# Half of the attention probabilities turned by VectorE's blocks and DMAs in place of TensorE

## The chip, the cores and the metric

The program runs on one core of a Trainium2 chip. The metric is the device time of one execution in microseconds (us). A core has five engines with an instruction queue each: TensorE (PE; its weight loads are shown as PEld), VectorE (DVE), ScalarE (ACT), GpSimd (POOL) and SyncE (SP, which here only issues DMAs). They run at the same time and wait for each other through semaphores. Operands lie in SBUF; TensorE writes to PSUM, from which ScalarE and VectorE copy ("evacuate").

## The reference

One layer of a decoder on a sequence of 256 positions and a width of 1024. One input projection feeds eight softmax attention heads of width 64 (MoBA) and four heads of gated linear attention (GLA); their outputs go through an output projection, then a feed-forward part with a short convolution (ConvGLU).

```python
xn = rms_norm(x, attn_norm_g[l])
proj = xn @ w_in[l]
mq = rope(split_heads(proj[..., o_mq:o_mk], MOBA_HEADS), pos)
mk = rope(split_heads(proj[..., o_mk:o_mv], MOBA_HEADS), pos)
mv = split_heads(proj[..., o_mv:o_gq], MOBA_HEADS)
y_moba = merge_heads(moba_attention(mq, mk, mv))
...
og = gla_attention(gq, gk, gv, split_heads(log_a, GLA_HEADS))
...
x = x + jnp.concatenate([y_moba, y_gla], axis=-1) @ w_out[l]
hn = rms_norm(x, ffn_norm_g[l])
h = causal_dwconv(hn @ w_ffn_up[l], conv_w[l], conv_b[l])
h_gate, h_val = h[..., :D_FF], h[..., D_FF:]
x = x + (jax.nn.silu(h_gate) * h_val) @ w_ffn_down[l]
return rms_norm(x, final_norm_g)
```

With 256 positions there is one key block, so the MoBA attention is plain causal softmax attention: for each head, P = softmax(q k^T / 8) below the diagonal, and P v.

## The kernel before

All large products are computed with operands split in a high part (`hi`) and a rest (`lo`), three matmuls each (`mm3`, lines 116 to 118). The weights come in slots of 1 MB: SP loads `raw`, ACT rounds it to `hi` (L99), DVE subtracts to get `lo` (L102), and a load is issued when a `raw` buffer has been split. The order of work in the first third of the kernel is written out by hand. The projection is a sequence of 48 steps on TensorE (`steps`, indices 0 to 47; from 24 on a step takes 1.4 us), and 16 more steps do the output projection. `plan` gives at an index q, or half a step later, a list of pieces that are emitted there: the attention's small matmuls, the work of ACT and DVE, and the splits of coming slots. PE, ACT and DVE each carry out their instructions in the emitted order.

The attention works on four pairs of heads. `m_scores(pr)` computes the scores of a pair on TensorE into two PSUM buffers of the pool `att` (four buffers, used in rotation). The same buffers hold one level of the GLA's triangular product (`lvl_c`), copied out by DVE in `lvl_d_` (L410). For each head h, `m_max(h)` (DVE, L557) adds the mask, takes the row maximum and writes the negated scores to one of four buffers `pes`; `m_exp(h)` (ACT, L564) takes the exponential and its sum; `m_div(h)` divides by the sum, with a reciprocal on DVE (L570), the first 128 columns scaled on ACT (L571) and the other 256 on DVE (L572). A head's P has 384 columns: rows are queries, two query blocks of 64 in each half of the partitions, and only the part up to the diagonal is kept.

P has to be turned for the product with v. `m_pt(pr)` does that on TensorE: twelve transposes of 64x128 pieces for a pair (L581) into two `att` buffers, evacuated by ACT in four operations (L587, L588) to `pt`. `m_av(n)` multiplies v and pt of two pairs (L601, L602) into one `att` buffer, which ACT and DVE split into `mh` and `ml` (L606, L607), operands of the output projection. `lvl_last` and `g_av` do the like for the GLA, `g_norm` and `g_gated` give its `y`, and `g_out` turns y on TensorE (L499).

Each pair passes through these steps one plan entry after another: m_scores(1), m_pt(0) and the softmax of heads 2 and 3 at 33.5; m_scores(2), m_pt(1) and heads 4 and 5 at 36.5; m_scores(3), m_pt(2) and heads 6 and 7 at 40; m_pt(3) and then m_av(0), m_av(1) at 45.5. Later in the kernel, `blocks` and `to_rows` (L913, L920) turn another tensor, hT, by 32x32 blocks on DVE and sixteen DMAs from SBUF to SBUF.

Of the kernel before, what the change touches and what calls it, by code (L numbers as in the profile page):

```python
# [34 lines left out]
def trunk_kernel(ctx: ExitStack, tc: tile.TileContext, xT_d, wG_d, w5_d, wo_d, up_d, dn_d,  # L35
                 par_d, gla_g_d, fin_g_d, wgu_d, cos_d, sin_d, causal_d, lvl_d, ident_d, out_d):
    nc = tc.nc
    V, A, T, DMA = nc.vector, nc.scalar, nc.tensor, nc.sync
# [123 lines left out]
    ml = main.tile([128, KT, S], F32R, name="ml")  # L162
# [66 lines left out]
    gv = at.tile([128, 2, 512], F32, name="gv")  # L229
# [8 lines left out]
    st = {}  # L238
# [310 lines left out]
    pes = [at.tile([128, 448], F32, name=f"pe{i}") for i in range(4)]  # L549
    for pe in pes:  # L550
        nc.gpsimd.memset(pe[64:128, 384:448], 0.0)

    def m_max(h):
        p, pe = st["s", h], pes[h % 4]
        mx = at.tile([128, 8], F32, name="mx", bufs=4)
        for i, (a, b, c) in enumerate(((0, 128, 0), (64, 320, 128))):
            V.tensor_tensor_reduce(pe[:, c:c + b - a], p[:, a:b], causal[:, c:c + b - a], -(HD ** -0.5), 3e38,  # L557
                                   ALU.add, ALU.min, mx[:, i:i + 1])
        st["mx", h] = mx
# [8 lines left out]
    def m_div(h):  # L568
        mx, pe = st["mx", h], st["pe", h]
        V.reciprocal(mx[:, 6:8], mx[:, 4:6])  # L570
        A.activation(pe[:, 0:128], pe[:, 0:128], AF.Copy, scale=mx[:, 6:7])  # L571
        V.tensor_scalar(pe[:, 128:384], pe[:, 128:384], mx[:, 7:8], None, op0=ALU.mult)  # L572

    def m_pt(pr):

        p = [att() for _ in range(2)]
        for h in range(2):
            for c in range(3):
                for r, rs in enumerate(HALVES):
                    a = c * 128 + 64 * (r and c > 0)  # L580
                    T.transpose(p[r][:, (3 * h + c) * 64:(3 * h + c) * 64 + 64],  # L581
                                st["pe", 2 * pr + h][rs, a:a + 128], ident[rs, rs])
        pt = at.tile([128, 2, 384], F32, name="pt", bufs=4)
        for r in range(2):
            o = pt.rearrange("p h (c t) -> p h c t", c=3)
            i = p[r][:, :384].rearrange("p (h c t) -> p h c t", h=2, c=3)
            A.activation(o[:, :, 0, HALVES[r]], i[:, :, 0], AF.Copy)  # L587
            A.activation(o[:, :, 1:, HALVES[1 - r]], i[:, :, 1:], AF.Copy)  # L588
        st["pt", pr] = pt

    def m_av(n):

        p = att()
        for pr in (2 * n, 2 * n + 1):
            c = S * (pr % 2)
            for hh in range(2):
                h = 2 * pr + hh
                pt = st["pt", pr][:, hh]
                r = slice(64 * hh, 64 * hh + 64)
                vs = slice(64 * h, 64 * h + 64)  # L600
                T.matmul(p[r, c:c + S], mv[:, 0, vs], pt[:, 0:256], start=True, stop=False, skip_group_check=True)  # L601
                T.matmul(p[r, c + 128:c + 256], mv[:, 1, vs], pt[:, 256:384],  # L602
                         start=False, stop=True, skip_group_check=True)
        mh = st["mh"]
        pv = p.rearrange("p (a t) -> p a t", a=2)
        A.activation(mh[:, 2 * n:2 * n + 2], pv, AF.Copy)  # L606
# [24 lines left out]
    for q, f in (  # L631
            (2, lambda: do((xsplit, 6), (xsplit, 7), (xsq, 3), (galloc, 6), (ghi, 6), (glo, 6), (ghi, 7), (glo, 7))),
            (4, lambda: do((xadd, 3), (xsum,), (hi, 6, 0), (lo, 6, 0), (g_wgs_hi,), (hi, 7, 0))),
            (12, lambda: do((xnorm, lambda: slots[7].split_lo(0, 512)), (lambda: slots[7].split_lo(512, 1024),), (g_evac, 0), (g_lr_split,), (g_evac, 1), (g_wgs_lo,), (hi, 7, 1), (lo, 7, 1))),
            (12.5, lambda: do((DMA.dma_start, lvl, lvl_d), (masks,))),
            (13.5, lambda: do((hi, 8, 0))),
            (14.5, lambda: do((g_transpose_lr,), (g_transpose, 0), (g_transpose, 1), (xrow,), (lo, 8, 0), (g_diag,))),
            (15.5, lambda: do((g_gate_mm,), (g_gate,), (hi, 9, 0), (g_decay,), (lo, 9, 0), (hi, 9, 1))),
            (16.5, lambda: do((lvl_u, 0), (lo, 9, 1), (lvl_u, 1))),
            (18, lambda: do((rope_a, 0, 0), (rope_b, 0, 0), (hi, 10, 0), (lo, 10, 0), (rope_a, 0, 1), (rope_b, 0, 1), (hi, 10, 1), (lo, 10, 1))),  # L640
            (20, lambda: do((hi, 11, 0), (lo, 11, 0), (hi, 11, 1), (lvl_keep,), (DMA.dma_start, glag, gla_g_d))),
            (24, lambda: do((lvl_u, 2), (rope_a, 1, 0), (rope_b, 1, 0), (lo, 11, 1), (rope_a, 1, 1), (rope_b, 1, 1), (hi, 12, 0), (lo, 12, 0), (g_diag2, 0), (g_diag2, 4))),
            (29, lambda: do((hi, 12, 1), (lvl_first,), (m_scores, 0), (m_max, 0), (m_exp, 0), (m_max, 1), (m_exp, 1), (lvl_d_, 0), (lvl_d_, 1), (lvl_u, 3), (m_div, 0), (m_div, 1), (lvl_d_, 2), (lo, 12, 1), (hi, 13, 0), (lo, 13, 0))),
            (33.5, lambda: do((hi, 13, 1), (m_scores, 1), (m_pt, 0), (m_max, 2), (m_exp, 2), (m_max, 3), (m_exp, 3), (lvl_u, 4), (m_div, 2), (m_div, 3), (lo, 13, 1), (lvl_d_, 3), (mv_evac, 0), (mv_evac, 1), (hi, 14, 0), (lo, 14, 0))),
            (36.5, lambda: do((hi, 14, 1), (m_scores, 2), (m_pt, 1), (m_max, 4), (m_exp, 4), (m_max, 5), (m_exp, 5), (lvl_u, 5), (m_div, 4), (m_div, 5), (lo, 14, 1), (lvl_d_, 4))),
            (37, lambda: do((hi, 15, 0), (lo, 15, 0))),
            (40, lambda: do((hi, 15, 1), (m_scores, 3), (m_pt, 2), (m_max, 6), (m_exp, 6), (m_max, 7), (m_exp, 7), (lvl_u64,), (lvl_d_, 5), (m_div, 6), (m_div, 7), (lvl_join,), (lo, 15, 1))),
            (41, lambda: do((gv_evac, 0), (gv_evac, 1), (hi, 16, 0), (lo, 16, 0))),
            (42, lambda: do((hi, 16, 1), (lo, 16, 1))),
            (45.5, lambda: do((m_pt, 3), (lvl_last,), (lvl_last_d,), (m_av, 0), (m_av, 1), (g_av, 0), (g_av, 1), (hi, 17, 0), (lo, 17, 0), (hi, 17, 1), (lo, 17, 1))),  # L650
            (48, lambda: do((g_tail,), (hi, 18, 0), (lo, 18, 0), (hi, 18, 1), (lo, 18, 1))),
            (51, lambda: do((g_out,),)),
            (52, lambda: do((A.preload_act_table_set, "abs_reciprocal_sqrt_and_small"), (hi, 19, 0), (lo, 19, 0), (hi, 19, 1), (lo, 19, 1)))):
        on(q, f)
# [55 lines left out]
    for q, (g, k) in enumerate(steps):  # L710
# [464 lines left out]
```

## Time and profile before

| | before |
|---|---|
| time, median of 3 executions | 306.48 us (306.25 to 307.33) |
| the profiled execution | 306.11 us |
| its span in the profile | 304.1 us |
| TensorE busy | 297.7 us |
| TensorE's granted clock | 1.00 |
| VectorE busy | 248.2 us |
| ScalarE busy | 207.0 us |
| DMA | 56.38 MB, 185 GB/s |

The span runs from the first to the last instruction that the profile shows; the execution's own time lies around it. In the rows of the profile, a group or a piece is named by its line (L102 is line 102 of the kernel before), its engine, its operation and its tiles, output first, with partitions x elements. A row of the view in order of time begins with the start in the span and the duration, both in us; "[0.64 <-ACT hi L99]" says that the engine was idle for 0.64 us before it and what ended that. "xN" merges N equal instructions in a row.

### The profile page before, as it was taken

The numbers are of one execution on the slowest core, as the hardware profiler recorded it, in microseconds if no ns is written. First come the engines' busy times: TensorE is split into PE (matmuls) and PEld (weight loads), VectorE is DVE, ScalarE is ACT, GpSimd is POOL, SyncE is SP. The second block draws the span as 40 slices with busy tenths as digits, with TensorE's granted clock in tenths as the row PEclk, the third lists the DMA queues.
The fourth block names the chain that finished last, engine by engine and source line by source line (L and its number), as shares of the span: only waits on it lengthen the run. The fifth ranks groups of instructions, "written<-read, shape, count | busy, mean of one in ns | idle before, by whom it ended". The sixth has DMA issues, their size and how long they took to land.

```text
span 304.1 us, 6224 instructions
## 1 busy us (share of the span) xinstructions
PE 297.7 (98%) x2470; PEld 282.2 (93%) x2470; DVE 248.2 (82%) x464; ACT 207.0 (68%) x384; POOL 4.8 (2%) x21
## 2 busy tenths in 40 slices
PE   8999999999999999999999999999999999999992
PEld 8999988777889999999999999999999999999992
DVE  3788998999387699799999998887888788876653
ACT  3988999898998487657667775555556665534362
POOL 2020000000000000000000000000000000000000
PEclk9999999999999999999999999999999999999999
DMA  6998845274553542991567666448788622220003
GB/s 163 391 332 307 297 165 198 91 261 141 176 182 134 204 168 65 426 370 32 210 245 256 254 235 236 170 156 224 211 194 234 267 71 69 71 69 2 0 0 139
DMA packets 20892, 56.38 MB, mean 185 GB/s; under 512 B 9840, under 2 KB 11648, under 8 KB 16640
## 3 DMA queue, kind: packets, MB, share of 16 engines
q1 hardware_dynamic: 20720, 55.86, 53.1%
q8 instruction: 19, 0.31, 0.4%
q10 hardware_dynamic: 144, 0.13, 0.1%
q14 instruction: 9, 0.07, 0.1%
HBM read 53.89 MB, written 1.05 MB: 181 GB/s over the span
## 4 chain that ended last, share of the span: by engine, by line
PE 98%; ACT 0%; issue 0%; DVE 0%; ACTq 0%
PE att L116 14%; PE att L117 14%; PE att L118 14%; PE acc L116 14%; PE acc L118 14%; PE acc L117 14%; PE att L746 4%; PE acc L727 1%; PE att L77 1%; PE att L399 1%; PE att L535 1%; PE att L581 1%; PE att L463 1%; PE att L601 1%; PE acc L735 1%; PE att L302 0%
## 5 line engine op out<-in xcount | busy, mean ns | idle before, releaser
L99 ACT ACTIVATE hi<-raw 128x1024 fp32r<-128x1024 f32 (+4 forms) x87 | 79.9, 941 | 38.4 <-PE att L117 31.9
L102 DVE TENSOR_TENSOR lo<-raw,hi 128x1024 fp32r<-128x1024 f32 (+4 forms) x89 | 93.6, 1065 | 14.0 <-ACT hi L99 14.0
L116 PE MATMUL att<-hh,hi 128*128 128x256 f32 x352 | 98.4, 279 | 0.0
L117 PE MATMUL att<-hl,hi 128*128 128x256 f32 x352 | 98.3, 279 | 0.0
L118 PE MATMUL att<-hh,lo 128*128 128x256 f32 x352 | 98.2, 279 | 0.0
L116 PEld LDWEIGHTS att<-hh,hi 128*128 128x128 f32 x352 | 66.2, 188 | 0.0
L117 PEld LDWEIGHTS att<-hl,hi 128*128 128x128 f32 x352 | 66.2, 188 | 0.0
L118 PEld LDWEIGHTS att<-hh,lo 128*128 128x128 f32 x352 | 66.2, 188 | 0.0
L873 DVE SCALAR_TENSOR_TENSOR c<-us,par,c 128x256 f32<-128x256 f32 x88 | 40.7, 482 | 4.1 <-ACT c L865 2.5
L865 ACT ACTIVATE c<-us,par 128x256 f32<-128x256 f32 x44 | 24.0, 591 | 23.7 <-DVE us L855 18.4
L118 PE MATMUL acc<-dhi,gl 128*128 128x512 f32 (+1 forms) x88 | 32.1, 365 | 0.0
L117 PE MATMUL acc<-dlo,gh 128*128 128x512 f32 (+1 forms) x88 | 32.1, 365 | 0.0
L116 PE MATMUL acc<-dhi,gh 128*128 128x512 f32 (+1 forms) x88 | 31.9, 363 | 0.0
L815 DVE TENSOR_TENSOR dlo<-draw,dhi 128x1024 fp32r<-128x1024 f32 x22 | 26.6, 1218 | 0.0
L855 DVE TENSOR_TENSOR us<-att,rb 128x512 f32<-128x512 f32 x20 | 13.8, 688 | 11.5 <-PE att L118 11.5
L810 ACT ACTIVATE dhi<-draw 128x1024 fp32r<-128x1024 f32 x22 | 23.0, 1046 | 0.0
L116 PE MATMUL acc<-hi,ah 128*128 128x512 f32 x48 | 19.5, 406 | 0.0
L118 PE MATMUL acc<-hi,al 128*128 128x512 f32 x48 | 19.0, 396 | 0.0
L117 PE MATMUL acc<-lo,ah 128*128 128x512 f32 x48 | 19.0, 396 | 0.0
L117 PEld LDWEIGHTS acc<-dlo,gh 128*128 128x128 f32 x88 | 16.5, 188 | 2.0
L116 PEld LDWEIGHTS acc<-dhi,gh 128*128 128x128 f32 x88 | 16.5, 188 | 1.9
L118 PEld LDWEIGHTS acc<-dhi,gl 128*128 128x128 f32 x88 | 16.5, 188 | 1.9
(222 smaller groups left out, 511.0 us busy)
## 6 DMA issues: line engine op xcount, KB each, us to landing
raw<-in_up SPq DMA_DIRECT2D x22, 1024.0 KB, 4.9
draw<-in_dn SPq DMA_DIRECT2D x22, 512.0 KB, 5.7
raw<-in_w SPq DMA_DIRECT2D x7, 1024.0 KB, 6.8
raw<-in_wo SPq DMA_DIRECT2D x4, 1024.0 KB, 4.8
raw<-in_w SPq DMA_DIRECT2D x4, 512.0 KB, 5.6
raw<-in_wG SPq DMA_DIRECT2D x3, 528.0 KB, 5.8
raw<-in_w SPq DMA_DIRECT2D x4, 256.0 KB, 5.4
xg<-hB SPq DMA_DIRECT2D x16, 64.0 KB, 6.4
```

What stands on the lines that cost most here:

```text
L77: T.matmul(wp[:, :w], zero, zero[:, :w], start=True, stop=True)
L99: A.activation(self.hi[:, a:b], self.raw[:, a:b], AF.Copy)
L102: V.tensor_sub(self.lo[:, a:b], self.raw[:, a:b], self.hi[:, a:b])
L116: T.matmul(out, sh, mh, start=first, stop=False, **kw)
L117: T.matmul(out, sh, ml, start=False, stop=False, **kw)
L118: T.matmul(out, sl, mh, start=False, stop=last, **kw)
L746: T.matmul(st["G"][tt][c][:, :c1 - c0], sta[:, k, tt * 128:(tt + 1) * 128], mov[:, kk, c0:c1], start=k == 0 and i == 0, stop=k == KT - 1 a ...
L810: A.activation(hi, downs[i][0], AF.Copy)
L815: V.tensor_sub(lo, d, hi)
L855: V.tensor_tensor(u[:, :, 2:], upo[i][2].rearrange("p (a t) -> p a t", a=2), rb[:, None, :].to_broadcast([128, 2, S]), op=ALU.mult)
L865: A.activation(cv[i][:, a], u[:, a, 2:], AF.Identity, bias=par[:, P_CB + m:P_CB + m + 1], scale=par[:, P_CW + 2 * 2 * NP + m:P_CW + 2 * 2 ...
L873: V.scalar_tensor_tensor(c[:, a], u[:, a, w:w + S], par[:, wc:wc + 1], c[:, a], op0=ALU.mult, op1=ALU.add)
```

## The change

The P of the first two pairs of heads (heads 0 to 3) is no longer turned by TensorE. In place of m_pt(0) and m_pt(1), `p_blocks(h)` transposes each 32x32 block of a head's P within its place on DVE, with one operation on 128x384 and one on 64x128 for the lower half, whose columns are shifted, and `p_turn` moves the blocks to their partitions with twenty DMAs from SBUF to SBUF, twelve with 48 KB and eight with 16 KB, in runs of 128 bytes, issued in turn from SP and from POOL, ten each. All eight transposes stand on DVE before the DMAs; the DMAs are issued after the transposes of head 3. The result goes to a new tile `pt4`, read by m_av(0). The queries of the last 128 columns come in another order there, so the split of m_av(0) into mh and ml is done in three pieces.

With it, the scaling of the 256 columns of heads 2, 3, 4 and 5 goes from DVE to ACT, and the plan entry with m_scores(3) and m_pt(2) goes from index 40 to 40.5. To make room, the new tile `tb` takes the buffer of `gqk`, and `AT01` that of `gk1`.

```diff
+    pt4 = at.tile([128, 12, 128], F32, name="pt4")
+    nc.gpsimd.memset(pt4.rearrange("p (h c) t -> p h c t", c=3)[64:128, :, 2, 64:128], 0.0)
+
+    def p_blocks(h):
+        if h == 0:
+            st["tb"] = at.tile([128, 50, 32], F32, name="tb", tag="gqk")
+        t = st["tb"][:, 12 * h:12 * h + 12].rearrange("p n b -> p (n b)")
+        V.transpose(t, pes[h][:, 0:384])
+        V.transpose(t[64:128, 64:192], pes[h][64:128, 0:128])
+
+    def p_turn():
+        n = 0
+        for b in range(4):
+            j = b // 2
+            for k in range(4):
+                src = st["tb"][32 * b:32 * b + 32]
+                dst = pt4[32 * k:32 * k + 32, :, 32 * b:32 * b + 32]
+                o = k + 2 * j
+                whole = j == 0 or k < 2
+                for c in ((None,) if whole else (0, 1)):
+                    q = (DMA, nc.gpsimd)[n % 2]
+                    n += 1
+                    if c is None:
+                        q.dma_start(dst, src[:, o:o + 45:4])
+                    else:
+                        q.dma_start(dst[:, c::3], src[:, o + 4 * c:o + 4 * c + 37:12])
...
-        V.tensor_scalar(pe[:, 128:384], pe[:, 128:384], mx[:, 7:8], None, op0=ALU.mult)
+        if h in (2, 3, 4, 5):
+            A.activation(pe[:, 128:384], pe[:, 128:384], AF.Copy, scale=mx[:, 7:8])
+        else:
+            V.tensor_scalar(pe[:, 128:384], pe[:, 128:384], mx[:, 7:8], None, op0=ALU.mult)
...
-        pt = at.tile([128, 2, 384], F32, name="pt", bufs=4)
+        pt = at.tile([128, 2, 384], F32, name="pt", bufs=2)
...
-                pt = st["pt", pr][:, hh]
+                pt = pt4[:, 3 * h:3 * h + 3].rearrange("p c t -> p (c t)") if n == 0 else st["pt", pr][:, hh]
...
-        A.activation(mh[:, 2 * n:2 * n + 2], pv, AF.Copy)
-        V.tensor_sub(ml[:, 2 * n:2 * n + 2], pv, mh[:, 2 * n:2 * n + 2])
+        for a, b, c in ((0, 256, 0),) if n else ((0, 128, 0), (128, 192, 192), (192, 256, 128)):
+            A.activation(mh[:, 2 * n:2 * n + 2, a:b], pv[:, :, c:c + b - a], AF.Copy)
+            V.tensor_sub(ml[:, 2 * n:2 * n + 2, a:b], pv[:, :, c:c + b - a], mh[:, 2 * n:2 * n + 2, a:b])
```

In the plan, m_pt(0) and m_pt(1) leave the entries 33.5 and 36.5, and the four p_blocks and p_turn stand in the entry 33.5 behind lvl_d_(3).

On TensorE, at index 33.5, the rows before are the GLA level and the scores of pair 1 (L399, L535), the twelve transposes of pair 0 (L581; `pe_153` and `pe_154` are heads 0 and 1) and the next projection step:

```order
L399 MATMUL att<-gqT,gkT 64x32 x16
L535 MATMUL att<-mkT,mqT 64x256 x2
L535 MATMUL att<-mkT,mqT 64x192 x2
L535 MATMUL att<-mkT,mqT 64x64 x2
L535 MATMUL att<-mkT,mqT 64x128 x2
L581 MATMUL att<-ident,pe_153 128x64 x6
L581 MATMUL att<-ident,pe_154 128x64 x6
L116 MATMUL acc<-hi,ah 128x512
```

Of the change, the same place on TensorE:

```order
L398 MATMUL att<-gqT,gkT 64x32 x16
L535 MATMUL att<-mkT,mqT 64x256 x2
L535 MATMUL att<-mkT,mqT 64x192 x2
L535 MATMUL att<-mkT,mqT 64x64 x2
L535 MATMUL att<-mkT,mqT 64x128 x2
L116 MATMUL acc<-hi,ah 128x512
```

The transposes are gone, and the projection follows on the scores; the entry 36.5 reads alike.

On VectorE, in the same entry, the rows before go from the softmax of heads 2 and 3 (`pe_155`, `pe_156`) over the copies of lvl_d_(3) and lo(14,0) to the first m_max of head 4:

```order
L570 RECIPROCAL mx<-mx 128x2
L572 TENSOR_SCALAR pe_155<-pe_155,mx 128x256
L570 RECIPROCAL mx<-mx 128x2
L572 TENSOR_SCALAR pe_156<-pe_156,mx 128x256
L102 TENSOR_TENSOR lo<-raw,hi 128x1024
L410 COPY_PREDICATED ATd<-lvl,att 128x4x4x8 x2
L102 TENSOR_TENSOR lo<-raw,hi 128x1024
L557 ISA pe_153,mx<-att,causal 128x128
```

Of the change, from the same reciprocals to the same m_max (the buffers' numbers are one lower):

```order
L597 RECIPROCAL mx<-mx 128x2 x2
L102 TENSOR_TENSOR lo<-raw,hi 128x1024
L409 COPY_PREDICATED ATd<-lvl,att 128x4x4x8 x2
L560 STREAM_TRANSPOSE tb<-pe_152 128x384
L561 STREAM_TRANSPOSE tb<-pe_152 64x128
L560 STREAM_TRANSPOSE tb<-pe_153 128x384
L561 STREAM_TRANSPOSE tb<-pe_153 64x128
L560 STREAM_TRANSPOSE tb<-pe_154 128x384
L561 STREAM_TRANSPOSE tb<-pe_154 64x128
L560 STREAM_TRANSPOSE tb<-pe_155 128x384
L561 STREAM_TRANSPOSE tb<-pe_155 64x128
L102 TENSOR_TENSOR lo<-raw,hi 128x1024
```

The two scalings have left, and eight transposes stand ahead of lo(14,0) and of m_max(4), which follows it as before.

On ScalarE, in the entry 36.5, the rows before are hi(14) (L99), the evacuation of pair 0 or 1 (L587, L588), the exponentials and the divisions of heads 4 and 5, and hi(15):

```order
L99 ACTIVATE hi<-raw 128x1024 x2
L587 ACTIVATE pt<-att 128x2x64
L588 ACTIVATE pt<-att 128x2x2x64
L587 ACTIVATE pt<-att 128x2x64
L588 ACTIVATE pt<-att 128x2x2x64
L564 ACTIVATE pe_153,mx<-pe_153,mx 128x128
L564 ACTIVATE pe_153,mx<-pe_153,mx 128x256
L564 ACTIVATE pe_154,mx<-pe_154,mx 128x128
L564 ACTIVATE pe_154,mx<-pe_154,mx 128x256
L571 ACTIVATE pe_153<-pe_153,mx 128x128
L571 ACTIVATE pe_154<-pe_154,mx 128x128
L99 ACTIVATE hi<-raw 128x1024 x2
```

Of the change, the same entry:

```order
L99 ACTIVATE hi<-raw 128x1024 x2
L591 ACTIVATE pe_152,mx<-pe_152,mx 128x128
L591 ACTIVATE pe_152,mx<-pe_152,mx 128x256
L591 ACTIVATE pe_153,mx<-pe_153,mx 128x128
L591 ACTIVATE pe_153,mx<-pe_153,mx 128x256
L598 ACTIVATE pe_152<-pe_152,mx 128x128
L600 ACTIVATE pe_152<-pe_152,mx 128x256
L598 ACTIVATE pe_153<-pe_153,mx 128x128
L600 ACTIVATE pe_153<-pe_153,mx 128x256
L99 ACTIVATE hi<-raw 128x1024 x2
```

The four evacuations have left, and two scalings of 128x256 have come (L600).

More of the change, by code (lines that the diff above doesn't have):

```diff
@@ L208, in trunk_kernel @@
     at = ap_.enter_context(tc.tile_pool(name="attn", bufs=1))
-    gqk = at.tile([128, 2, NG], F32, name="gqk")
+    gqk = at.tile([128, 2, NG], F32, name="gqk", tag="gqk")
     gqT = at.tile([128, 2, S], F32, name="gqT")
     gkT = at.tile([128, 2, S], F32, name="gkT")
-    gk1 = at.tile([128, 2, S], F32, name="gk1")
+    gk1 = at.tile([128, 2, S], F32, name="gk1", tag="gk1")
     q1 = at.tile([128, 256], F32, name="q1")
@@ L218, in trunk_kernel @@
     AT = at.tile([128, 8, 128], F32, name="ATf")
-    AT01 = at.tile([128, 4, 128], F32, name="AT01")
     wgs = at.tile([128, 256], F32R, name="wgs")
@@ L439, in lvl_last_d @@
     def lvl_last_d():
+        AT01 = st["AT01"] = at.tile([128, 4, 128], F32, name="AT01", tag="gk1")
         for h in range(2):
@@ L460, in g_av @@
             if tt == 1:
-                T.matmul(o, AT01[:, pr * 2 + hh], gv[:, 0, vs], start=True, stop=False)
+                T.matmul(o, st["AT01"][:, pr * 2 + hh], gv[:, 0, vs], start=True, stop=False)
             i = (pr * 2 + tt) * 2 + hh
@@ L643, in trunk_kernel @@
             (29, lambda: do((hi, 12, 1), (lvl_first,), (m_scores, 0), (m_max, 0), (m_exp, 0), (m_max, 1), (m_exp, 1), (lvl_d_, 0), (lvl_d_, 1), (lvl_u, 3), (m_div, 0), (m_div, 1), (lvl_d_, 2), (lo, 12, 1), (hi, 13, 0), (lo, 13, 0))),
-            (33.5, lambda: do((hi, 13, 1), (m_scores, 1), (m_pt, 0), (m_max, 2), (m_exp, 2), (m_max, 3), (m_exp, 3), (lvl_u, 4), (m_div, 2), (m_div, 3), (lo, 13, 1), (lvl_d_, 3), (mv_evac, 0), (mv_evac, 1), (hi, 14, 0), (lo, 14, 0))),
-            (36.5, lambda: do((hi, 14, 1), (m_scores, 2), (m_pt, 1), (m_max, 4), (m_exp, 4), (m_max, 5), (m_exp, 5), (lvl_u, 5), (m_div, 4), (m_div, 5), (lo, 14, 1), (lvl_d_, 4))),
+            (33.5, lambda: do((hi, 13, 1), (m_scores, 1), (m_max, 2), (m_exp, 2), (m_max, 3), (m_exp, 3), (lvl_u, 4), (m_div, 2), (m_div, 3), (lo, 13, 1), (lvl_d_, 3), (p_blocks, 0), (p_blocks, 1), (p_blocks, 2), (p_blocks, 3), (p_turn,), (mv_evac, 0), (mv_evac, 1), (hi, 14, 0), (lo, 14, 0))),
+            (36.5, lambda: do((hi, 14, 1), (m_scores, 2), (m_max, 4), (m_exp, 4), (m_max, 5), (m_exp, 5), (lvl_u, 5), (m_div, 4), (m_div, 5), (lo, 14, 1), (lvl_d_, 4))),
             (37, lambda: do((hi, 15, 0), (lo, 15, 0))),
-            (40, lambda: do((hi, 15, 1), (m_scores, 3), (m_pt, 2), (m_max, 6), (m_exp, 6), (m_max, 7), (m_exp, 7), (lvl_u64,), (lvl_d_, 5), (m_div, 6), (m_div, 7), (lvl_join,), (lo, 15, 1))),
+            (40.5, lambda: do((hi, 15, 1), (m_scores, 3), (m_pt, 2), (m_max, 6), (m_exp, 6), (m_max, 7), (m_exp, 7), (lvl_u64,), (lvl_d_, 5), (m_div, 6), (m_div, 7), (lvl_join,), (lo, 15, 1))),
             (41, lambda: do((gv_evac, 0), (gv_evac, 1), (hi, 16, 0), (lo, 16, 0))),
```

## The prediction

> **What bounds the kernel now.** First the page's busy times and its chain of work that ended last, then the busy time by stretch, then each engine's rows in order of time around the change.
>
> ```profile
> span 304.1 us, 6224 instructions
> ...
> PE 297.7 (98%) x2470; PEld 282.2 (93%) x2470; DVE 248.2 (82%) x464; ACT 207.0 (68%) x384; POOL 4.8 (2%) x21
> ...
> PE 98%; ACT 0%; issue 0%; DVE 0%; ACTq 0%
> ```
>
> TensorE is busy for 297.7 of 304.1 us and is 98% of the chain, so work taken from it is worth its full length, as long as it never has to wait. By stretch (columns: length, then PE, PEld, DVE, ACT, POOL):
>
> ```profile
> 57.00:66.00 9.00, 9.00 (x144) 7.10 (x143) 8.29 (x24) 8.92 (x23) 0.00 (x0) 1.00 0.46 136
> 66.00:73.00 7.00, 7.00 (x84) 5.55 (x83) 6.92 (x29) 6.07 (x21) 0.00 (x0) 1.00 0.51 184
> 73.00:82.00 9.00, 9.00 (x100) 7.14 (x100) 5.89 (x14) 8.35 (x24) 0.21 (x2) 1.00 0.52 192
> ```
>
> The average hides this: where the change is made, DVE is busy for 8.29 of 9 us and then 6.92 of 7, and ACT for 8.92 of 9 and later 8.35 of 9. Neither has room to give there. TensorE never waits for them now, but by how little is read from the rows below.
>
> **What TensorE loses.** Two of the four m_pt steps go; the chain of waits shows each as one piece:
>
> ```profile
> 58.57 0.53 PE att L581 x12
> 64.65 0.53 PE att L581 x12
> ```
>
> 2 x 0.53 = 1.06 us less on TensorE. That is 0.34% of the time, and all that the change can gain; a measurement of this kernel can tell about 0.5% from no change (1.5 us: under 305.0 or over 308.0).
>
> **What VectorE gets.** Eight block transposes, between the copies of lvl_d_(3) and lo(14,0). The nearest rows are the four of 128x512 later in this kernel, and for the effect of size the elementwise operations of 256 and 128:
>
> ```profile
> L913 DVE STREAM_TRANSPOSE hB<-xg x4: 703/704/707, 175.3 to 199.1; 128x512 f32<-128x512 f32 x4
> ...
> 73.16 0.42 DVE L370 TENSOR_TENSOR gkT<-gkT,dec 128x256 f32<-128x256 f32 x1
> 73.68 0.29 DVE L373 TENSOR_TENSOR q<-gqT,dec 128x128 f32<-128x128 f32 x1
> 73.89 0.28 DVE L374 TENSOR_TENSOR k<-gkT,dec 128x128 f32<-128x128 f32 x1
> ```
>
> 128 more columns cost 0.13 us (0.42 - 0.29), so 128x384 takes about 0.704 - 0.13 = 0.57 us and 64x128 about 0.29. The second overwrites part of what the first wrote and starts after its end; the next head's may start 0.21 us after it (73.68 to 73.89). A head: 0.57 + 0.03 + 0.21 = 0.81 us; four: **3.2 us**. Bounds: strictly by columns, with every overlap, 4 x (0.53 + 0.18 - 0.16) = 2.2; with the 512 price for the first and no overlap at all, 4 x (0.70 + 0.29 + 0.1) = 4.4. I take 3.2, from the row of the same operation.
>
> What it does to the stretch, from DVE's rows before:
>
> ```profile
> 62.02 0.35 DVE L572 TENSOR_SCALAR pe<-pe,mx 128x256 f32<-128x256 f32 x1
> 62.29 0.16 DVE L570 RECIPROCAL mx<-mx 128x2 f32<-128x2 f32 x1
> 62.75 1.22 DVE L102 TENSOR_TENSOR lo<-raw,hi 128x1024 fp32r<-128x1024 f32 x1
> 63.88 0.49 DVE L410 COPY_PREDICATED ATd<-lvl,att 128x128 f32<-128x128 int32 x2
> 65.01 1.23 DVE L102 TENSOR_TENSOR lo<-raw,hi 128x1024 fp32r<-128x1024 f32 x1 [0.64 <-ACT hi L99]
> 66.15 0.28 DVE L557 CUSTOM_DVE_ANT_0 pe<-att,causal 128x128 f32<-128x128 f32 x1
> ```
>
> The scalings of heads 2 and 3 leave DVE, 0.27 us each (62.02 to 62.29): 0.54. The 0.64 us of idle time before lo(14,0) takes up another part. 3.2 - 0.54 - 0.64 = 2.0: m_max(4) starts at 68.15 in place of 66.15.
>
> **What that does to ScalarE.** It issues in a written order, so a late m_max holds all behind it:
>
> ```profile
> 66.66 0.43 ACT L564 ACTIVATE pe<-pe,mx 128x128 f32<-128x128 f32 x1
> 67.05 0.54 ACT L564 ACTIVATE pe<-pe,mx 128x256 f32<-128x256 f32 x1
> 67.45 0.23 ACT L564 ACTIVATION_READ_ACCUMULATOR pe<-pe,mx 128x1 f32 x1
> 68.42 0.76 ACT L571 ACTIVATE pe<-pe,mx 128x128 f32<-128x128 f32 x2
> 69.08 1.99 ACT L99 ACTIVATE hi<-raw 128x1024 fp32r<-128x1024 f32 x2
> 72.00 0.28 ACT L587 ACTIVATE pt<-att 128x128 f32<-128x128 f32 x1 [0.93 <-PE att L581]
> ...
> 74.68 0.87 ACT L571 ACTIVATE pe<-pe,mx 128x128 f32<-128x128 f32 x2
> ...
> 77.89 1.99 ACT L99 ACTIVATE hi<-raw 128x1024 fp32r<-128x1024 f32 x2
> 80.42 0.28 ACT L587 ACTIVATE pt<-att 128x128 f32<-128x128 f32 x1 [0.53 <-PE att L581]
> 80.59 0.38 ACT L588 ACTIVATE pt<-att 128x256 f32<-128x256 f32 x1
> ```
>
> ACT is rid of the eight evacuations of pt for pairs 0 and 1, but the room falls into a wait: m_exp(4) starts 0.28 us after m_max(4), at 68.4 (66.66 before, +1.75). Four 128x256 scalings come to ACT, 0.40 us each (67.05 to 67.45); those of heads 2 and 3 fall before that wait and cost nothing while it lasts, those of heads 4 and 5 add 0.8. So hi(15) starts at 71.6, not 69.08, and the evacuation of m_pt(2) at 73.6, not 72.0: 1.75 + 0.8 - 0.93 of former idle time = 1.6 late. DVE's lo(15,0) waits for hi(15), and through it m_max(6) to m_div(6), some 2.1 us late: 76.8 for 74.68. From there ACT runs through. hi(16) ends at 79.9 + 2.0 = 81.9; the 0.53 us that ACT waited for TensorE before m_pt(3) is used up. The first half of the evacuation of m_pt(3) ends 0.55 us after it starts: **82.4 for 80.97**.
>
> **Where TensorE then waits.** The att pool has four PSUM buffers in rotation, and m_av(0) takes the one that this half empties:
>
> ```profile
> 81.03 0.23 PE L436 MATMUL att<-q,gkT 64*64 64x64 f32 x2
> 81.19 0.66 PE L601 MATMUL att<-pt,mv 128*64 128x256 f32 x4
> ```
>
> Before, m_av(0) started at 81.19, 0.2 us after that buffer was free; TensorE came from L436 with no gap. Now it starts at about 82.5, **1.3 us later**. The 1.06 us saved is spent in waits on the way: scores(3) is put half a step later, and m_pt(2) now takes the buffers of scores(2) and so waits for lvl_d_(4), which DVE reaches late; together about 1 us, and the rest at m_av(0). The sum is one for one in the turn: 2.2 us there gives +0.3, 4.4 gives +2.5. The scaling's price on ACT, between 0.27 (DVE's) and 0.54 (its full duration), moves it by 0.3 either way.
>
> **What I cost at nothing.** The twenty transfers. The nearest rows are the turn of hT, 64 KB in runs of 128 bytes like these:
>
> ```profile
> L920 SPq DMA_DIRECT2D xg<-hB x16: 597/720/847, 202.2 to 229.2; - x16
> ...
> DMA to landing us min/median/max: 5.7/6.4/7.3
> ```
>
> They start when the blocks are done, at 67.0, and are due at 82.4: 15.4 us. SP issues ten: 10 x 0.72 + 6.4 = 13.6 us, hidden. No row shows a DMA issued by POOL. From SP's price it is hidden too; bounds by SP's extremes 10 x 0.60 + 5.7 = 11.7 and 10 x 0.85 + 7.3 = 15.8 (0.4 us late). At (15.4 - 6.4) / 10 = 0.9 us an issue the cover ends.
>
> The weight loads queued behind the ten on SP (the third and fourth of wo) go out some 3 us later; the third is first read at 92.24, over 10 us after it lands. The split of mh and ml of m_av(0) in three makes ACT and DVE take turns:
>
> ```profile
> 83.00 0.59 ACT L606 ACTIVATE mh<-att 128x512 fp32r<-128x512 f32 x1
> 84.09 0.60 ACT L606 ACTIVATE mh<-att 128x512 fp32r<-128x512 f32 x1 [0.50 <-PE att L602]
> ...
> 91.81 1.29 DVE L491 TENSOR_TENSOR y<-y,gr 128x512 f32<-128x512 f32 x2 [0.18 <-ACT gr L452]
> ...
> 94.56 0.71 PE L499 MATMUL att<-ident,y 64*128 64x64 f32 x16
> ```
>
> About 1 us of turns against 0.5 us of former idle time leaves ACT some 0.6 us later than TensorE; y was ready at 93.1, TensorE read it at 94.56, so 1.4 us cover it. After that TensorE is bound by itself, and the shift stays.
>
> **Rivals.** (1) The lag is smaller than I add up, and the saving stays: TensorE 1.06 us shorter, 306.5 - 1.1 = **305.4**. It needs the turn at about 1 us, or idle time on ACT that I missed; for it speaks only that PE is 98% of the chain, against it that ACT is busy for 8.92 of 9 us in the first stretch.
> (2) POOL's issues are slower than SP's and set m_av(0): from 0.9 us each on. At 1.2 us: 67.0 + 12 + 6.4 = 85.4, 4.2 us after 81.19: **310.7**. For it: the price is shown by no row, the cover is thin. Against it: POOL is free, and the 6.4 us to landing were measured behind weight loads on the same queue. A harder form: POOL is held up whenever DVE works. DVE idles 0.1 of 7 us and 3.1 of 9 in the stretches from 66 to 82, so of the 7.2 us of issues some 4 would be left at 82; with landing, m_av(0) at 92, **317**. No row has a transfer issued by POOL beside DVE, so I leave it 0.05 of this rival's chance.
>
> For the price of an issue, the Trainium skill ("DMA: Bandwidth & Descriptors", Latency and other measured facts) gives about 1 us to the first byte for a transfer that POOL issues; an estimate by that and its fixed 2 us to landing is 67 + 10 + 2 = 79, hidden. For the harder form, the skill ("SBUF — State Buffer", SBUF: two separate sides) says that VectorE locks POOL out of writing descriptors, but only during operations in a two-port mode, such as copies and tensor_scalar. Of these DVE keeps only two L572 before 82 us, 0.35 us each, so by that narrower rule the hold is 0.7 us and hidden; nothing in this profile shows either.
>
> (3) The split covers less than I say and y is late for TensorE: another 0.5 us, **308.3**.
>
> **The numbers.** The profiled execution took 306.1 us, 2.0 more than its span; its forecast is 306.1 + 1.3 = 307.4. It lies 0.4 below the median of the runs, so on 306.48: **307.8**. Chances: this forecast 0.50 (two fifths of it, with a turn over 3.4 us, past 308.0), rival 1 0.18, rival 2 0.27, rival 3 0.05. Faster by over 0.5%: 0.03, the part of rival 1 that gains more than its sum. Slower: 0.20 + 0.27 + 0.02 = 0.49. Within 0.5%: 0.48. The range 305.4 to 310.7 takes in the turn's bounds (306.8 to 309.0), rival 1 and half of rival 2. Slower or no change is nearly all of it; of the forecast alone the range is 306.8 to 309.0.
>
> **What would show it.** Right: eight DVE transposes of 3.2 us in all; m_max(4) near 68; TensorE idle before m_pt(2) and before m_av(0), the latter released by ACT's evacuation of pt; m_av(0) near 82.5. Wrong: m_av(0) released by a DMA (rival 2), or TensorE busy throughout with m_av(0) near 80.1 (rival 1), or a wait at L499's transposes (rival 3).

## The result, and the profile after

The changed kernel takes 308.01 us (median of 7 runs, 307.91 to 309.19) and the kernel before 306.11 us beside it (7 runs, 305.69 to 307.33). The ratio is 1.0062, with a 95% interval of 1.0044 to 1.0081: **1.9 us slower**, between 1.3 and 2.5. The forecast was 1.3 us slower; on the 306.48 us shown with the kernel before it said 307.8. One execution among the runs below was slow, at a granted clock of 0.75 (e1, 366.95 us), and is left out of the ratios.

The profiled execution of the changed kernel is the slowest of its seven, 309.19 us with a span of 307.4. The page of the changed kernel, its span, busy times and the chain that ended last:

```profile
span 307.4 us, 6221 instructions
...
PE 296.4 (96%) x2446; PEld 280.3 (91%) x2446; DVE 250.6 (82%) x470; ACT 207.0 (67%) x382; POOL 10.8 (4%) x32
...
PE 82%; DVE 7%; ACT 6%; issue 2%; DMA 2%; SPq 1%; DVEq 0%; ACTq 0%
```

TensorE does less, but the chain now leaves it for DVE and ACT. The view of waits, TensorE's alone (line that waited, what released it, us in total, times, longest); ahead of it the one such row of the kernel before:

```profile
PE att L77 <- PEq L1164: 0.8, 1, 0.8
```

```profile
PE acc L758 <- ACT hi L99: 1.5, 2, 1.0
PE att L631 <- ACT pt L618: 1.2, 1, 1.2
PE att L398 <- DVE dec L363: 0.8, 1, 0.8
PE att L77 <- PEq L1195: 0.8, 1, 0.8
PE att L611 <- DVE ATd L409: 0.6, 1, 0.6
```

Three waits are new in the stretch of the change: 0.8 at m_scores(3) (L398), 0.6 at m_pt(2) (L611), 1.2 at m_av(0) (L631), 2.6 us against 1.06 saved. The first of them is at the GLA level that m_scores(3) begins with. The 1.5 at L758 are not the change's: they lie within the first 10 us, where this execution waited for its first weights. How much of it arrives is read where both kernels still run the same rows, TensorE's first scores of m_scores(1), before and after:

```profile
57.83 0.75 PE L535 MATMUL att<-mkT,mqT 64*64 64x256 f32 x16
```

```profile
58.64 0.75 PE L535 MATMUL att<-mkT,mqT 64*64 64x256 f32 x16
```

So 0.81 us are to be taken off every time of the profile after. VectorE, in order of time:

```profile
64.59 0.57 DVE L560 STREAM_TRANSPOSE tb<-pe 128x384 f32<-128x384 f32 x1
65.19 0.31 DVE L561 STREAM_TRANSPOSE tb<-pe 64x128 f32<-64x128 f32 x1
65.52 0.58 DVE L560 STREAM_TRANSPOSE tb<-pe 128x384 f32<-128x384 f32 x1
...
68.03 0.31 DVE L561 STREAM_TRANSPOSE tb<-pe 64x128 f32<-64x128 f32 x1
68.38 1.23 DVE L102 TENSOR_TENSOR lo<-raw,hi 128x1024 fp32r<-128x1024 f32 x1
69.52 0.28 DVE L584 CUSTOM_DVE_ANT_0 pe<-att,causal 128x128 f32<-128x128 f32 x1
```

The turn takes 68.38 - 64.59 = 3.79 us. Each operation starts only when the one ahead of it has ended, also from one head to the next (65.19 + 0.31, then 65.52). m_max(4) stands at 69.52 - 0.81 = 68.71, 2.56 us later than before (66.15). ScalarE behind it:

```profile
69.85 0.40 ACT L591 ACTIVATE pe<-pe,mx 128x128 f32<-128x128 f32 x1 [2.31 <-DVE mx L584]
...
73.00 1.99 ACT L99 ACTIVATE hi<-raw 128x1024 fp32r<-128x1024 f32 x2
74.90 0.25 ACT L617 ACTIVATE pt<-att 128x128 f32<-128x128 f32 x1
...
78.19 0.87 ACT L598 ACTIVATE pe<-pe,mx 128x128 f32<-128x128 f32 x2 [0.59 <-DVE mx L597]
...
81.41 1.99 ACT L99 ACTIVATE hi<-raw 128x1024 fp32r<-128x1024 f32 x2
83.30 0.26 ACT L617 ACTIVATE pt<-att 128x128 f32<-128x128 f32 x1
83.45 0.37 ACT L618 ACTIVATE pt<-att 128x256 f32<-128x256 f32 x1
```

ACT idles 2.31 us for m_max(4) and then runs on almost without a gap to the evacuation of m_pt(3). m_av(0) takes the buffer that its first half empties:

```profile
83.88 0.66 PE L631 MATMUL att<-pt,mv 128*64 128x256 f32 x4 [1.16 <-ACT pt L618]
```

83.88 - 0.81 = 83.07 against 81.19 before: 1.88 us, as much as the medians differ by, and the transposes of y, at 97.25 for 94.56, are late by the same. (The three waits less 1.06 would give only 1.5. From the scores shown above to m_av(0), TensorE idles 2.55 us and its busy time falls by 0.67, from 23.36 to 22.69, not by 1.06; 0.16 of the rest is in m_pt(2), which takes 0.75 us after its wait for 0.59 before. Where the other 0.2 is, the rows do not say.) The transfers do not show up in it. The groups of the tile tb (durations as min/median/max in ns, first and last start in us):

```profile
L576 SPq DMA_DIRECT2D pt<-tb x6: 585/610/741, 68.0 to 72.9; - x6
L576 POOL DMA_DIRECT2D pt<-tb x6: 615/616/739, 68.3 to 72.6; - x6
L578 POOL DMA_DIRECT2D pt<-tb x4: 548/554/562, 71.5 to 73.7; - x4
L578 SPq DMA_DIRECT2D pt<-tb x4: 598/638/682, 71.5 to 74.2; - x4
...
DMA to landing us min/median/max: 1.9/2.7/3.5
```

POOL's issues take 0.55 to 0.62 us and at most 0.74, no more than SP's, beside a DVE that is busy for 5.30 of these 6.20 us (68.0 to 74.2); the last transfer is issued at 74.2 and has landed some 6 us before m_av(0).

### The profile page after: what moved, and what is told of

The parts are those of the page before. It is cut to its first block, busy times and chain, and to the rows that moved or that the text cites. A ratio compares the mean times of both kernels' runs of the same rounds, so it can differ in the third digit from the quotient of the medians.

```text
span 307.4 us, 6221 instructions
## 1 busy us (share of the span) xinstructions
PE 296.4 (96%) x2446; PEld 280.3 (91%) x2446; DVE 250.6 (82%) x470; ACT 207.0 (67%) x382; POOL 10.8 (4%) x32
## 3 DMA queue, kind: packets, MB, share of 16 engines
HBM read 53.89 MB, written 1.05 MB: 179 GB/s over the span
## 4 chain that ended last, share of the span: by engine, by line
PE 82%; DVE 7%; ACT 6%; issue 2%; DMA 2%; SPq 1%; DVEq 0%; ACTq 0%
PE att L116 14%; PE att L117 14%; PE att L118 14%; PE acc L116 11%; PE acc L117 10%; PE acc L118 10%; PE att L777 3%; DVE lo L102 2%; DMA raw<-in_w 2%; ACT hi L99 2%; ACT pe L591 1%; PE acc L758 1%; DVE pe L584 1%; DVE ATd L409 1%; ACT qs L512 1%
## 5 line engine op out<-in xcount | busy, mean ns | idle before, releaser
L99 ACT ACTIVATE hi<-raw 128x1024 fp32r<-128x1024 f32 (+4 forms) x87 | 79.9, 942 | 39.0 <-PE att L117 31.3
```

Source lines behind the costliest of these rows:

```text
L99: A.activation(self.hi[:, a:b], self.raw[:, a:b], AF.Copy)
```

## The experiments

Theory A was that the turn, 3.8 us and not 3.2, arrives at m_av(0) through m_max(4), m_exp(4) and ACT's written order, and that all else of the change is covered. Twelve kernels were run; where zeros stand for the turned P, TensorE does the same work on them.

**The transfers alone, the turn alone, half of the turn, TensorE's saving undone.** Four edits of the changed kernel:

```diff
 e1_no_transfers:  -(p_turn,)
 e2_no_turn:       -(p_blocks, 0), (p_blocks, 1), (p_blocks, 2), (p_blocks, 3), (p_turn,)
 e3_half_turn:     -(p_blocks, 2), (p_blocks, 3), (p_turn,)
 e8_pe_back:       +(m_ptx, 0) behind m_scores(1), +(m_ptx, 1) behind m_scores(2)
```

where `m_ptx` is the twelve transposes of m_pt without the evacuation.

> The twenty transfers are left out (the probabilities of the first two pairs that go into m_av(0) are zeros from a memset); the eight block transposes on VectorE stay. Theory A (the turn on VectorE is 3.8 us long and reaches m_av(0) through m_max(4), m_exp(4) and ScalarE one for one, the transfers are covered): 308.0 us, between 307.7 and 308.3, the turn's rows as in the changed kernel (0.94 us a head) and m_av(0) waiting about 1.2 us for the evacuation of m_pt(3) as there. Theory B (part of the 0.6 us beyond the forecast comes from the transfers, by the queues, by the later wo loads or by VectorE slowed): 307.0 to 307.5, with a shorter wait somewhere.

> The eight block transposes and the twenty transfers are left out (zeros go into m_av(0)); everything else of the change stays: m_pt(0) and m_pt(1) off TensorE, four scalings on ScalarE, the split of mh and ml. Theory A: the chain over VectorE is free again, only TensorE's saving of two m_pt (1.06 us) is left of the kernel before's 306.1: 305.1 us, between 304.8 and 305.5, m_av(0) without a wait. Theory C (the two moved scalings and the split on ScalarE make part of the lateness by themselves): 305.8 to 306.5, with 0.5 us or more of wait at m_av(0) or at the first matmul on wo.

> Only heads 0 and 1 are turned (four transposes, 1.9 us), no transfers, zeros go into m_av(0). Theory A, one for one: 308.0 less 1.9 is 306.1, between 305.8 and 306.5. Theory D (a threshold: VectorE's queue has slack, and only the last microsecond of the turn costs): the same 305.1 as without the turn, or the full 308.0 if the first transposes do it.

> The changed kernel with the transposes of m_pt(0) and m_pt(1) put back on TensorE (24 transposes into att banks that nobody reads), nothing evacuated. Theory A (m_av(0) stands where VectorE's and ScalarE's chain puts it, TensorE waits 2.6 us on the way, so its saving of 1.06 us never reaches the end): 308.0 to 308.3, TensorE's waits before m_av(0) shorter by about 1 us in sum. Theory E (TensorE's saving does count, in full, and what the turn takes away stands apart from it): 309.1.

| kernel | us (range, runs) | ratio to before (95%) | from the first scores of m_scores(1) to m_av(0), us |
|---|---|---|---|
| kernel before | 305.86 (305.64 to 306.44, 23) | 1 | 23.36 |
| changed kernel | 308.01 (307.91 to 309.19, 7) | 1.0062 (1.0044 to 1.0081) | 25.24 |
| e1, no transfers | 308.06 (307.80 to 308.39 and one at 366.95, 6) | 1.0068 (1.0055 to 1.0081) | 25.24 |
| e2, no turn | 306.00 (305.75 to 307.03, 11) | 1.0005 (0.9996 to 1.0013) | 23.48 |
| e3, half of the turn | 306.04 (305.61 to 306.91, 11) | 1.0007 (0.9998 to 1.0015) | 23.47 |
| e8_pe_back | 308.19 (307.79 to 309.17, 6) | 1.0078 (1.0065 to 1.0091) | 25.25 |

The last column is read from one trace each, in the same way as above; for e1 from these rows:

```profile
57.71 0.75 PE L535 MATMUL att<-mkT,mqT 64*64 64x256 f32 x16
82.95 0.66 PE L631 MATMUL att<-pt,mv 128*64 128x256 f32 x4 [1.16 <-ACT pt L618]
```

The kernel before stood beside the four edits in these runs; beside the changed kernel it took 306.11. e1 and e8_pe_back came out as theory A has it. The transfers are covered. TensorE's saving is worth nothing in this kernel: giving it back costs 0.2 us by the medians and 0.4 against the kernel before beside each, less than these runs tell apart, and leaves m_av(0) in its place, while TensorE's waits ahead of it fall by about 1 us, from 2.6 to these two (L640 is m_av(0) there, L620 m_pt(2)):

```profile
PE att L640 <- ACT pt L627: 1.2, 1, 1.2
PE att L620 <- DVE ATd L409: 0.4, 1, 0.4
```

e3 has the time that theory A gave, but not for its reason: e2 has the same, so for e2 theory A falls and theory C holds. Half of the turn costs nothing at all, the other half 2.0 us (theory D, with another level); and **without any turn the saving is still not there**. VectorE in e2, where the turn stood:

```profile
63.16 0.49 DVE L409 COPY_PREDICATED ATd<-lvl,att 128x128 f32<-128x128 int32 x2
65.57 1.23 DVE L102 TENSOR_TENSOR lo<-raw,hi 128x1024 fp32r<-128x1024 f32 x1 [1.93 <-ACT hi L99]
```

VectorE has 1.93 us of idle time there, not the 0.64 of the kernel before, because ScalarE brings hi(14) 0.8 us late and DVE has lost two scalings. Half of the turn (1.9 us) all but fills it; in e3 0.17 us are left. What lies beyond it is paid in full: 3.79 - 1.93 = 1.86, and between e3 and e1 m_av(0) moves by 1.77. And in e2's view of waits TensorE still stops at m_av(0):

```profile
PE att L631 <- ACT pt L618: 1.1, 1, 1.1
```

The 1.06 us are saved and given back there. So ScalarE makes m_av(0) late without VectorE's help.

**Who holds the saving back.** Two more kernels without the turn, one with the four scalings back on DVE, one with hi(16) and lo(16) behind the evacuation of m_pt(3), which needs ACT earlier than TensorE needs hi(16):

```diff
 e4_no_turn_scale:  e2 and
-        if h in (2, 3, 4, 5):
+        if h in ():
 e6_no_turn_hi16:   e2 and
-(41, ... (gv_evac, 1), (hi, 16, 0), (lo, 16, 0)), (42, ... (hi, 16, 1), (lo, 16, 1))
+(41, ... (gv_evac, 1)), (45.5, ... (m_av, 0), (hi, 16, 0), (lo, 16, 0), (m_av, 1), (hi, 16, 1), (lo, 16, 1), ...
-(48, ... (g_tail,), ...
+(48, ... (g_tail,), (hi, 17, 1), (lo, 17, 1), ...
```

> As in the run without the turn (no block transposes, no transfers, zeros go into m_av(0)), and the four scalings of heads 2 to 5 back on VectorE. There, TensorE got its two m_pt back and gave 1.09 us away again at m_av(0), where the evacuation of m_pt(3) on ScalarE came late: hi(14) stood on ScalarE 0.8 us later than before against the start of the stretch. Theory C (the moved scalings make ScalarE late by about 0.8 us and take the saving): ScalarE's m_div(6) about 1.2 us earlier, m_av(0) waits less than 0.5 us, 304.9 to 305.4. Theory F (ScalarE is at its limit there with or without the scalings, or the entry moved from 40 to 40.5 makes it late): still 305.8 to 306.1 with a wait of about 1.1.

> As the run without the turn (scalings on ScalarE; no block transposes, no transfers, zeros go into m_av(0)), but hi(16) and lo(16), which TensorE needs only two and a half steps later, stand behind the evacuation of m_pt(3) on ScalarE; half of hi(17) goes behind g_tail. Theory C (the whole saving of TensorE is there and is held up only by ScalarE at m_av(0)): no wait at m_av(0), 304.9 to 305.2. Theory F (something else holds TensorE, so that the saving shows nowhere): 305.8 to 306.1.

e4 took 305.35 us (305.08 to 305.93, 10 runs; ratio 0.9979, 0.9969 to 0.9988), e6 305.00 (304.79 to 305.77, 5 runs; 0.9970, 0.9958 to 0.9982); the kernel before 305.94 beside them. e6 has no wait at m_av(0), which stands 22.31 us after the first scores, 1.05 us earlier than in the kernel before. In e4 it stands at 22.60; m_div(6) is 0.9 us earlier there than in e2 (16.92 us for 17.79 after the first scores), not the 1.2 expected, and this is left of the wait:

```profile
PE att L631 <- ACT pt L618: 0.2, 1, 0.2
```

Theory C holds, theory F falls. TensorE's saving is real: 0.9 us of the 1.06 by the times (0.6 to 1.3), and in e6's trace all of it at m_av(0), of which 0.4 goes again before the transposes of y (13.78 us from m_av(0) to there, for 13.37). Two things on ScalarE take it away together, and undoing either brings most of it back: the scalings that were moved there to relieve VectorE (0.7 us: e2 is 0.14 over the kernel before beside it, e4 0.59 under), and hi(16) in front of the evacuation that TensorE waits for.

**The same cure with the turn in.** e5_hi16_later is the changed kernel with e6's order; e7_spread also turns heads 2 and 3 only after lo(14,1), puts lvl_d_(4) ahead of m_div(4), and m_av(0) behind m_av(1) and g_av; e8_spread_gr is e7 with another order on ACT:

```diff
 e7_spread:
-(33.5, ... (p_blocks, 0), (p_blocks, 1), (p_blocks, 2), (p_blocks, 3), (p_turn,), (mv_evac, 0), ...
+(33.5, ... (p_blocks, 0), (p_blocks, 1), (mv_evac, 0), ...
-(36.5, ... (lvl_u, 5), (m_div, 4), (m_div, 5), (lo, 14, 1), (lvl_d_, 4)
+(36.5, ... (lvl_u, 5), (lvl_d_, 4), (m_div, 4), (m_div, 5), (lo, 14, 1), (p_blocks, 2), (p_blocks, 3), (p_turn,)
+(45.5, ... (m_av, 1), (hi, 16, 0), (lo, 16, 0), (g_av, 0), (g_av, 1), (m_av, 0), (hi, 16, 1), (lo, 16, 1), (hi, 17, 0), ...
 e8_spread_gr, against e7:
+(45.5, ... (g_av, 0), (g_av, 1), (hi, 16, 1), (lo, 16, 1), (hi, 17, 0), (m_av, 0), (lo, 17, 0)
```

> The changed kernel, turn and transfers in, with hi(16) and lo(16) behind the evacuation of m_pt(3) in the same way. Of the changed kernel's three waits on TensorE (0.78 at m_scores(3), 0.62 at m_pt(2), 1.16 at m_av(0)) the last goes, the first two stay. Theory A (waits add up along TensorE): 308.0 less 1.2 is 306.8, between 306.6 and 307.1. Theory G (the work moved behind makes y or the hi of wo late instead): 307.5 to 308.5, with a new wait at the transposes of y or at the first matmul on wo.

> A version meant to keep the saving: heads 0 and 1 are turned where all four were, heads 2 and 3 only behind m_max(4), m_max(5), lvl_u(5), lvl_d_(4) and lo(14,1) on VectorE; the transfers therefore start about 5 us later, and m_av(0) stands behind m_av(1) and g_av; hi(16) and lo(16) behind the evacuation of m_pt(3). Theory A (the half of the turn that has no idle time of VectorE is moved to where nothing of TensorE's path waits for it): no wait over 0.3 us before the output projection, 305.0 to 305.5. Theory H (VectorE has no room anywhere in this stretch: m_max(6) and the evacuation of m_pt(3) come late by the same 1.9 us and TensorE waits at m_pt(3) or m_av(1)): 306.5 to 307.5. Theory I (the transfers, now due within 10 us, come late for m_av(0)): a wait there for a DMA, over 306.

e5 took 308.49 us (307.62 to 310.22, 6 runs; ratio 1.0080, 1.0059 to 1.0101), no better than the changed kernel and outside theory A. Its profiled execution is the fastest of the six; there no wait is new, as theory G would have it, m_av(0) stands at 24.64 for the changed kernel's 25.24, and its wait is 0.55 in place of 1.16:

```profile
82.09 0.66 PE L631 MATMUL att<-pt,mv 128*64 128x256 f32 x4 [0.55 <-ACT pt L618]
```

That rest is not the evacuation, though the view names it: the half that m_av(0) needs had ended at 81.26. e10 below has the same 0.55 us, put down there to a load of weights. In e6, without the transfers, TensorE does not stop there, and in e7 and e8_spread_gr, with them, it does not either; what it waits for is open. What its other executions wait for no trace shows, so e5 does not decide between the theories. e7 took 309.86 (309.05 to 310.20, 4 runs; 1.0120, 1.0105 to 1.0134), outside all three theories. TensorE waits for no DMA there, against theory I. All three waits of the stretch are gone but for 0.4 us, and another has come in their place:

```profile
PE acc L116 <- ACT gr L452: 2.5, 1, 2.5
```

The output projection needs the accumulators that gr leaves, and ACT evacuates gr (L452) behind m_av(0)'s late evacuation, hi(16) and hi(17).

> The spread turn again, mended: in the run before it TensorE's waits ahead of the output projection were down to 0.4 us, but the evacuation of gr on ScalarE, which frees TensorE's accumulators, had come behind m_av(0)'s late evacuation, hi(16) and hi(17), and cost 2.5 us. Here hi(16,1) and hi(17,0) stand ahead of m_av(0)'s evacuation, in the 2.5 us in which ScalarE waited for it. Theory A (that wait was the whole of the loss, and the turn itself now costs nothing): gr's evacuation 1.7 to 2 us earlier, wait for it under 0.7 us, 305.0 to 306.0. Theory H (VectorE has no room for the turn wherever it stands): 307 or more, with a wait on VectorE's lo or on pt.

> The kernel before with the same order of m_av, g_av, hi(16) and hi(17) and nothing else of the change: what the order alone is worth. The kernel before has no wait on TensorE in this stretch, so theory A expects no gain: 305.7 to 306.3. Theory J (what the mended version gains comes from the order, not from the turn): under 305.5.

e8_spread_gr took 306.64 (306.30 to 307.47, 8 runs; 1.0017, 1.0005 to 1.0030). The wait for gr is down to 0.6. It is 1.4 us better than the changed kernel and still 0.5 slower than the one before, between the ranges of its two theories. Theory H falls by the trace: TensorE waits neither for lo nor for pt, so VectorE has room for the whole turn when it is spread. Theory A's sum is short: the attention starts 0.94 us earlier than in the kernel before (its first product, now m_av(1), 22.42 us after the first scores for 23.36), but TensorE then takes 14.62 us to the transposes of y for 13.37. Of these 1.25 us, 0.6 are the wait for gr, and 0.4 the price of the order itself: e9, which has it and no wait there, takes 13.78. The rest is open. The order alone, e9 in the kernel before, gives 306.27 (305.86 to 306.83, 11 runs; 1.0006, 0.9997 to 1.0015; before 306.12 beside both): no gain, as theory A has it, since TensorE waited for nothing there; the 0.4 us are too little for these runs. No version with the turn beat the kernel before; the spread turn with the four scalings back on VectorE was not run.

**The split of mh and ml.**

```diff
 e10_unsplit:
-        for a, b, c in ((0, 256, 0),) if n else ((0, 128, 0), (128, 192, 192), (192, 256, 128)):
+        for a, b, c in ((0, 256, 0),):
```

> The changed kernel with mh and ml of m_av(0) evacuated in one piece again (the columns of its heads then stand in another order than the output projection takes them). Theory A (the split is covered: y is there before the transposes that read it): 307.8 to 308.2 as the changed kernel. Rival 3 of the prediction (the split makes y late): 307.4 to 307.7.

309.16 us (308.30 to 309.56, 5 runs; 1.0094, 1.0079 to 1.0109), slower than either theory has it, so the time decides nothing. The trace does. The transposes of y in the changed kernel and in e10:

```profile
L499 PE MATMUL att<-ident,y x16: 221/222/272, 97.2 to 97.7; 64*128 64x64 f32 x16
```

```profile
L499 PE MATMUL att<-ident,y x16: 221/222/272, 97.1 to 97.6; 64*128 64x64 f32 x16
```

m_av(0) starts at 83.88 in the one and at 83.78 in the other: the same 13.3 to 13.4 us from there to y, with and without the split, and as many as in the kernel before (81.19 to 94.56). It is covered. What made e10 slow is in the section on the hardware.

**The end of the program.**

```diff
 e11_one_pool:  e2 and
+(nc.gpsimd.dma_start, pt4[0:32, 0, 0:32], ident[0:32, 0:32])
```

> As the run without the turn (no block transposes, zeros go into m_av(0)), with one transfer of 4 KB on POOL's queue, out of the identity matrix into a corner of pt4, at the place of the twenty. In the seven profiled runs without the transfers the span ends 2.8 to 2.9 us behind ScalarE's last issue of an output, in the six with them 3.4 to 3.5. Theory K (any use of POOL's own queue makes the end of the program longer, whatever it carried): 3.4 to 3.5 us here, and 306.0 plus 0.5 is 306.5. Theory L (the tail goes with the number of the transfers or with what SP carries): 2.8 to 2.9, and 306.0.

306.23 us (305.96 to 307.21, 11 runs; 1.0006, 0.9997 to 1.0015), and the span ends 304.5 - 301.56 = 2.9 us behind ScalarE's last issue: theory L. It is not the use of POOL's queue as such.

## Why the prediction was nearly right

Its mechanism held step by step, and each step is late by 0.5 to 0.6 us against the forecast, once the 0.81 us are taken off: m_max(4) 68.7 for 68.15, hi(15) 72.2 for 71.6, the evacuation of m_pt(2) 74.1 for 73.6, m_div(6) 77.4 for 76.8, the first half of m_pt(3)'s evacuation done at 83.0 for 82.4, m_av(0) at 83.1 for 82.5. TensorE waits at m_pt(2) and m_av(0), released by what was said; the wait at m_scores(3), 0.8 us for the `dec` of lvl_u(5) on VectorE, the forecast had only as half a step's delay. That 307.8 lies so near to 308.01 is in part luck: the base of 306.48 was 0.37 above the 306.11 of the kernel before beside it, which hides most of the 0.6.

- **The mis-sized term: the turn, 3.2 us, measured 3.79.** Its parts were right (0.57 and 0.29 forecast, 0.57 and 0.31 measured). Wrong was "the next head's may start 0.21 us after it": the next head starts 0.33 us after, when the 64x128 operation has ended, and lo(14,0) too. One for one this gives 1.3 + 0.59 = 1.9, the measured loss.
- **One for one holds only from 1.9 us of turn on.** The prediction took the sum as linear and put the saving at 305.4 for a turn of about 1 us (rival 1). With no turn at all it is 306.0, and with half of it the same. The step that failed there is that idle time on VectorE was read from the kernel before, 0.64 us; the scalings moved to ACT make it 1.93, and the same scalings hold TensorE at m_av(0). The forecast came out because the turn is longer than that idle time and so hides the scalings: ACT waits 2.31 us for m_max(4). The forecast said so of the scalings of heads 2 and 3 ("cost nothing while it lasts"), but not what they do when the wait is short.
- **TensorE's saving, 1.06 us:** shown real by e6 (0.9 us, 1.05 at m_av(0)), and shown worthless in this order by e8_pe_back.
- **The transfers:** at m_av(0) of the changed kernel they cost nothing, as forecast. They land in 1.9 to 3.5 us, not the 6.4 taken from hT's, and POOL's price is 0.55 to 0.62 us an issue (0.74 at most), against the 0.9 from which rival 2 would have set in. VectorE is busy for 5.30 of the 6.20 us beside them, which refutes the rival's harder form. "SBUF — State Buffer" of the Trainium skill (SBUF: two separate sides), weighed in the prediction, would hold POOL only in VectorE's two-port modes; no tensor_scalar and no copy from SBUF to SBUF ran on VectorE during these 6 us, so the trace does not test that narrower rule.
- **The split (rival 3):** covered, as e10's trace shows.

## What to carry to other kernels

Where two or three engines are all near full, the idle time that a change leans on must be read from the kernel without the costly part, not from the kernel before: here another edit of the same change made the idle time, and took the gain. To free the engine that bounds a kernel may bring nothing, as here in e2, until the next engine's queue has been put in order of what is needed first; ask what stands in front of the row that releases the bound engine. And the turn by 32x32 blocks was a chain here: count each transpose at its full duration, one after the other.

## What the hardware showed

**The clock can fall in a stretch with waits.** In e10's trace the granted clock (the third number from the end of each row; the others are length, busy times and DMA) drops in the middle of the kernel:

```profile
68.00:70.00 2.00, 1.73 (x8) 1.06 (x6) 2.00 (x11) 1.17 (x5) 2.00 (x5) 1.00 0.61 109
70.00:72.00 2.00, 1.24 (x48) 1.10 (x48) 1.80 (x7) 2.00 (x9) 2.00 (x4) 1.00 0.73 133
72.00:74.00 2.00, 1.64 (x14) 1.38 (x15) 1.36 (x4) 2.00 (x4) 1.42 (x5) 0.78 0.57 104
74.00:76.00 2.00, 2.00 (x6) 1.61 (x5) 2.00 (x12) 2.00 (x11) 0.00 (x0) 0.50 0.53 101
76.00:78.00 2.00, 2.00 (x9) 1.57 (x9) 1.90 (x11) 1.34 (x5) 0.00 (x0) 0.87 0.92 381
```

It follows TensorE's two waits at m_scores(3) and m_pt(2) and costs 2 us x 0.22, 0.50 and 0.13 in the last three rows, 1.7 us of clock, of which a shorter wait at m_av(0) (0.55 for 1.16) gave 0.6 back. The 1.1 us left are about what e10 is slower by than the changed kernel (1.15; m_av(0) stands 26.16 us after the first scores for 25.24). The other thirteen traces show the clock low only after TensorE's last matmul, and the changed kernel, e1 and e5 have the same two waits and no such drop; so the waits alone do not bring it. The Trainium skill ("TensorE: Matmul & The Clock Gate", Part 1: The HAM clock gate) has a gate that halves the clock after an idle window of about 3.4 us, counted in windows that run on by themselves. Half the clock for about one such window agrees with e10 (0.50 from 73.4 to 76.2, and back at 1.00 from 76.6); an idle window does not, since TensorE was busy for 1.24 and 1.64 of 2 us just ahead. Windows that run on by themselves would also make it a matter of chance which execution is hit. The mean clocks of whole executions bear on this: the kernel before lies at 0.994 to 0.999 beside all the edits, and three of e10's five (309.16 to 309.56 us), the slowest of e5 (310.22) and all four of e7 at 0.988 to 0.993; but e10's other two, at 0.994 and 0.996, also take longer than the changed kernel's median (308.30 and 308.85), and e7's trace shows no drop. So the drop is shown for e10's one trace, and for the spread of the other kernels it is not.

**The end of the program.** SP's last issue of an output, before and after:

```profile
301.14 0.45 SPq L1107 DMA_DIRECT2D out_y<-yy  x1
```

```profile
303.97 0.42 SPq L1138 DMA_DIRECT2D out_y<-yy  x1
```

From its end to the end of the span it is 304.1 - 301.59 = 2.5 us before and 307.4 - 304.39 = 3.0 after. All eight traces without the twenty transfers show 2.46 to 2.55, all six with them 2.95 to 3.15. One transfer on POOL is not enough for it (e11). The medians of e1 and the changed kernel, 308.06 and 308.01, do not show this half microsecond: e1's executions last 2.1 to 2.2 us longer than their spans, the changed kernel's 1.8. Why the time outside the span differs, and what the half microsecond is, stay open.
